# Sums of weights for a seven-product scheme on one Trainium2 core: one accumulating DMA and GpSimd additions in place of three accumulating DMAs, with the feed-forward in three parts

## The chip, the core and the metric

The kernel runs on one core of a Trainium2 chip. The metric is the device time of one execution in microseconds; for a comparison several executions are timed and their median is taken. Beside the timed runs, one execution is recorded by the hardware profiler; every line number and duration below is from that record. Engines are TensorE (PE, with its weight loads PEld), VectorE (DVE), ScalarE (ACT), GpSimd (POOL) and SyncE (SP), each with a queue of its own that is worked off in order.

## What is computed

A decoder trunk of two layers on 512 tokens of width 1024, all in float32. Each layer is a feed-forward, a token mixer and a second feed-forward, added to the residual stream. The change concerns the four feed-forwards only:

```
def swiglu(h, w_gate, w_up, w_down):
    return (jax.nn.silu(h @ w_gate) * (h @ w_up)) @ w_down

for l in range(2):
    x = x + 0.5 * swiglu(rms_norm(x, ffn1_norm[l]), ffn1_w_gate[l], ffn1_w_up[l], ffn1_w_down[l])
    ...                       # mixer: causal convolution and differential attention
    x = x + 0.5 * swiglu(rms_norm(x, ffn2_norm[l]), ffn2_w_gate[l], ffn2_w_up[l], ffn2_w_down[l])
```

The hidden width is 2816, which is 22 tiles of 128.

## The kernel before, in words

The residual stream x lies in SBUF with features on partitions: eight tiles (KT) of 128 features by 512 tokens. Every product is made from split operands: a value is rounded to a shorter float (hi) and its remainder kept (lo), and three matmuls, hi·hi, hi·lo and lo·hi, stand for one (`mm3`, lines 136 to 142). Weights are split on the chip: `parts_of` (93 to 95) lets ScalarE write hi (L94) and VectorE write lo (L95).

A feed-forward (`ffn`, 341 to 401) goes through its 22 hidden tiles in two halves of 11. For each tile it makes gate and up outputs, applies silu and the product, and splits the result into `hh` and `hl` (`gated`, L358 and L359). After 11 tiles comes a down pass: for each of the 8 output tiles, 11 hidden tiles times three matmuls accumulate in a bank `ps_d`, which L399 adds to x. Its weights come in chunks of eight blocks of 128x128 (L397).

The first three tiles (PLAIN) are made by plain products. The other 19 tiles of a feed-forward, a pair of gate and up each, go through `seven` (304 to 339): the pair's 2 by 2 block product is made from seven products in place of eight, each over four feature tiles, so 7 × 4 × 3 = 84 matmuls of 256 tokens. It needs sums of weight blocks (g1, g2 are the halves of the gate weights, u1, u2 of the up weights): g1, g2, u2, g1+u1, u2+u1, g1+u2+u1, and the sum of all four; the signs are in the activations and in the last step. It also needs sums of activations, made once a feed-forward by `Halves` (267 to 302): whole normalized tiles `hn`, sums `ht` by GpSimd (L284, L285) and VectorE, split into `th` and `tl`; `settle` splits the whole tiles into `acth` and `actl`. Each of the seven products goes to a quarter of two PSUM banks: a and d are halves of the first, c and b of the second. Between the products the running sum of a bank's half is copied out by ScalarE (L323 to L329) or added by VectorE (L331 to L338) to tiles `g` and `n` in SBUF.

The sums of weights are made by `sums` (109 to 134). SP loads g1 and u2 into one buffer `raw`, which is split; then GpSimd issues a DMA that adds u1 to both halves in the buffer (`add_into`, L107), which is split again; a second accumulating DMA adds g1 to one half, which is split; a third adds g2 to it, which is split. So a pair has three accumulating DMAs, each changing a buffer that must have been read. The buffers are rings: three `wraw` of 128x1024, of which a pair takes one, four `whi` and four `wlo`, of which a pair takes three each; and two smaller ones each for g2 (`wraw2`, `whi2`, `wlo2`).

The order of instructions on each engine is fixed at build time by a scheduler that works with modelled durations; only the first matmul of each of the seven products is pinned to its place. An engine waits at its next instruction until what this one needs is there, whatever stands behind it. Bank pairs for the seven products take turns through three tags (`pair_banks`, 262 to 264), one of which (`mm`) also gives the two `ps_d` banks.

## Time and profile before

| | |
|---|---|
| time, median of 3 runs | 2290.9 us (2290.48 to 2295.74) |
| the profiled execution | 2303.2 us, of which 2301.1 us are its span |
| TensorE busy, mean granted clock | 1940.3 us (84%), 0.942 of full speed |
| VectorE, ScalarE, GpSimd busy | 1182.6, 917.9, 595.9 us |
| DMA | 236.49 MB, 103 GB/s over the span |
| accumulating DMAs on GpSimd's queue | 228: 76 of 512 KB, 152 of 256 KB |
| chain that ended last | PE 39%, DMA 30% (loads and accumulations of gate and up weights), DVE 13%, ACT 6%, issue 6% |

How to read the lines that follow. A group of the profile reads: line, engine, operation, output<-inputs, shapes, count | busy us and mean ns of one | idle time of the engine just before these instructions and what ended it. A line of waits reads: engine, tile and line that waited <- what it waited for: us in total, times, longest. A line of a timeline reads: start in us from the span's start, duration, engine, line, operation, [idle before <- what ended it]. A line of windows reads: stretch, length, busy time of PE, PEld, DVE, ACT and POOL with counts, granted TensorE clock (PEclk), DMA share, GB/s. Matmuls overlap one another, so that the time from one start to the next, not the duration, is the pace.

### The profile page before, as it was taken

The page shows a single profiled execution, that of the slowest core. Times are in us where ns is not written, and L with a number is a line of the kernel's source. Part 1 is how long each engine was busy: PE and PEld are TensorE (multiplying, and loading weights), DVE is VectorE, ACT ScalarE, POOL GpSimd, SP SyncE. Part 2 cuts the span into 40 slices and gives each one's busy share as a digit, 9 for nine tenths or more (in the row PEclk, how much of TensorE's full clock was granted, in tenths as well). Part 3 has the DMA queues.
Part 4 walks back from the last instruction along what each step waited for, and adds up shares of the span by engine and source line. Part 5 has one row for each costly group of instructions (what it writes and reads, how often), then busy time and mean ns, then how long its engine had stood idle before and what let it go on. Part 6 is the DMA issues. An engine that isn't in the chain of part 4 may idle for free.

```text
span 2301.1 us, 28742 instructions
## 1 busy us (share of the span) xinstructions
PE 1940.3 (84%) x11124; PEld 1703.9 (74%) x11124; DVE 1182.6 (51%) x1848; ACT 917.9 (40%) x1532; POOL 595.9 (26%) x500
## 2 busy tenths in 40 slices
PE   7678877899998879777987797679999987897789
PEld 5667776788787768767877687677887867777677
DVE  7444344548869443344474443444488674424442
ACT  5333233335745342333433322333458444313331
POOL 4110111119934110111121101121397421101110
PEclk9799999999998999899998999999999999999899
DMA  5455365532213554455425544555321245535542
GB/s 158 111 120 126 76 123 103 136 101 83 83 37 83 115 120 108 98 110 115 128 60 109 115 121 83 118 104 133 95 87 56 65 91 111 128 92 106 108 105 89
DMA packets 104088, 236.49 MB, mean 103 GB/s; under 512 B 11271, under 2 KB 11430, under 8 KB 103952
## 3 DMA queue, kind: packets, MB, share of 16 engines
q0 software_dynamic: 44192, 82.51, 22.6%
q1 hardware_dynamic: 59616, 152.07, 21.3%
q8 instruction: 87, 1.43, 0.2%
q14 instruction: 49, 0.40, 0.1%
q10 hardware_dynamic: 144, 0.08, 0.0%
HBM read 232.51 MB, written 3.42 MB: 103 GB/s over the span
## 4 chain that ended last, share of the span: by engine, by line
PE 39%; DMA 30%; DVE 13%; issue 6%; ACT 6%; POOL 0%; ACTq 0%; POOLq 0%; SPq 0%; DVEq 0%
DMA wraw<-in_gu 30%; DVE wlo L95 7%; PE ps_d L138 6%; PE ps_d L142 6%; PE ps_d L141 6%; ACT whi L94 6%; PE ps_pair L318 6%; PE ps_pair L141 2%; PE ps_pair L142 2%; PE ps_pair L138 2%; PE ps_pair L518 1%; PE ps_pair L517 1%; PE ps_pair L516 1%; PE ps_out L141 1%; PE ps_sc L634 1%
## 5 line engine op out<-in xcount | busy, mean ns | idle before, releaser
L95 DVE TENSOR_TENSOR wlo<-wraw,whi 128x512 fp32r<-128x512 f32 (+1 forms) x506 | 500.5, 993 | 657.1 <-ACT whi L94 645.4
L94 ACT ACTIVATE whi<-wraw 128x1024 fp32r<-128x1024 f32 (+1 forms) x550 | 467.8, 873 | 891.3 <-DMA wraw<-in_gu 539.9
L107 POOL DMA_DIRECT2D wraw<-in_gu x228 | 223.4, 981 | 1277.1 <-DVE wlo L95 1198.4
L318 PE MATMUL ps_pair<-acth,whi 128*128 128x256 f32 x1216 | 373.8, 307 | 151.7 <-DVE g L331 138.9
L318 PE MATMUL ps_pair<-th,whi 128*128 128x256 f32 x912 | 293.4, 322 | 158.1 <-ACT n L325 76.7
L318 PEld LDWEIGHTS ps_pair<-acth,whi 128*128 128x128 f32 x1216 | 255.8, 210 | 167.2 <-ACT whi L94 130.9
L318 PE MATMUL ps_pair<-actl,whi 128*128 128x256 f32 x1216 | 367.9, 303 | 10.2 <-DVE actl L295 10.2
L318 PE MATMUL ps_pair<-acth,wlo 128*128 128x256 f32 x1216 | 366.1, 301 | 0.3 <-DVE wlo L95 0.3
L318 PEld LDWEIGHTS ps_pair<-th,whi 128*128 128x128 f32 x912 | 196.3, 215 | 184.8 <-ACT n L325 87.3
L138 PE MATMUL ps_d<-hh,whi 128*128 128x512 f32 x704 | 276.0, 394 | 16.4 <-ACT whi L94 13.8
L318 PE MATMUL ps_pair<-tl,whi 128*128 128x256 f32 x912 | 280.3, 307 | 10.5 <-DVE tl L289 10.5
L318 PE MATMUL ps_pair<-th,wlo 128*128 128x256 f32 x912 | 277.4, 304 | 0.2 <-DVE wlo L95 0.2
L141 PE MATMUL ps_d<-hl,whi 128*128 128x512 f32 x704 | 274.7, 390 | 0.0
L142 PE MATMUL ps_d<-hh,wlo 128*128 128x512 f32 x704 | 273.3, 390 | 0.0
L318 PEld LDWEIGHTS ps_pair<-actl,whi 128*128 128x128 f32 x1216 | 256.6, 211 | 13.4 <-DVE actl L295 12.4
L318 PEld LDWEIGHTS ps_pair<-acth,wlo 128*128 128x128 f32 x1216 | 256.6, 211 | 0.6 <-DVE wlo L95 0.5
L318 PEld LDWEIGHTS ps_pair<-tl,whi 128*128 128x128 f32 x912 | 196.0, 215 | 14.0 <-DVE tl L289 13.6
L318 PEld LDWEIGHTS ps_pair<-th,wlo 128*128 128x128 f32 x912 | 195.1, 214 | 0.7 <-DVE wlo L95 0.7
L138 PEld LDWEIGHTS ps_d<-hh,whi 128*128 128x128 f32 x704 | 132.5, 188 | 50.9 <-ACT whi L94 18.9
L142 PEld LDWEIGHTS ps_d<-hh,wlo 128*128 128x128 f32 x704 | 132.7, 189 | 27.5
L141 PEld LDWEIGHTS ps_d<-hl,whi 128*128 128x128 f32 x704 | 132.5, 188 | 26.2
L138 PE MATMUL ps_pair<-acth,whi 128*128 128x512 f32 x320 | 125.6, 397 | 6.0 <-ACT whi L94 6.0
(175 smaller groups left out, 2880.9 us busy)
## 6 DMA issues: line engine op xcount, KB each, us to landing
wraw<-in_gu SPq DMA_DIRECT2D x232, 256.0 KB, 3.5
wraw<-in_dn SPq DMA_DIRECT2D x88, 512.0 KB, 3.9
wraw<-in_gu POOLq DMA_DIRECT2D x76, 512.0 KB, 6.1
wraw<-in_gu POOLq DMA_DIRECT2D x152, 256.0 KB, 4.2
wraw<-in_wqkv SPq DMA_DIRECT2D x24, 512.0 KB, 3.6
wraw<-in_gu SPq DMA_DIRECT2D x22, 512.0 KB, 3.6
wraw<-in_wag SPq DMA_DIRECT2D x16, 512.0 KB, 3.7
wraw<-in_wout SPq DMA_DIRECT2D x16, 512.0 KB, 3.6
```

The source lines that it names most:

```text
L94: S.activation(hi, raw, AF.Copy)
L95: (eng or V).tensor_tensor(out=lo, in0=raw, in1=f32(hi), op=ALU.subtract)
L107: nc.gpsimd.dma_start(dst, src, accum_op=ALU.add)
L138: first = T.matmul(ps, wh, xh, start=start, stop=False)
L141: T.matmul(ps, wh, xl, start=False, stop=False)
L142: T.matmul(ps, wl, xh, start=False, stop=stop)
L318: mm = T.matmul(ps, l, r, start=first and i == j == 0, stop=False, skip_group_check=True)
L516: T.matmul(ps[n], xh[:, t], wh, start=k == 0, stop=False)
L517: T.matmul(ps[n], xh[:, t], wl, start=False, stop=False)
L518: T.matmul(ps[n], xl[:, t], wh, start=False, stop=k == KT - 1)
L634: T.matmul(scs[m], qz[:, m, h, tq], kt[:, h, :W], start=True, stop=True)
```

## The change

Three things are changed, all in the feed-forwards.

The sums. A pair now loads g whole (`whole`), g1 and u2 into a second buffer (`two`), and u2 once more into the small ring. One accumulating DMA adds u1 to both halves of `two`. GpSimd then makes g1+u2+u1 and the sum of all with two `tensor_tensor` additions into a third buffer (`more`). A pair takes three `wraw` buffers, of which there are now five. Splits are in another order: whole (g1, g2), u2u1, g1u2u1, u2, all, g1u1.

The parts. The 22 tiles go in three parts of 8, 8 and 6 tiles with a down pass after each. The array of down weights in memory stays laid out for two halves of 11, so `gather` puts a chunk of eight blocks together from two to four loads (a few chunks are one load). Temporary sums `ht` of `Halves` take turns in two buffers in place of four.

The products. Their order becomes g1, u2u1, g2, g1u2u1, u2, all, g1u1, with b and c exchanged in the second bank. The sums of products and the gate are made in the PSUM banks by VectorE, and silu and the split read them there.

In the changed kernel, line numbers are higher: L95 becomes L97 and L94 L96, L107 becomes L140, the additions are L145 and L146, the matmuls L318 become L343, the copies of a, c, a, d out of the banks are L348, L350, L353 and L355, and loads of down weights are L117.

```diff
@@ -40,6 +40,8 @@
 STATS_AT = 5
 
 PLAIN = 3
+
+PARTS = ((0, 8), (8, 8), (16, 6))
 HS = SEQ // 2
 
 SPACE = 392
@@ -84,7 +86,7 @@
         return psum.tile([P, 512], F32, tag=tag, name=name, bufs=BANKS[tag])
 
 
-    RING = {"wraw": 3, "whi": 4, "wlo": 4, "wraw2": 2, "whi2": 2, "wlo2": 2}
+    RING = {"wraw": 5, "whi": 4, "wlo": 4, "wraw2": 2, "whi2": 2, "wlo2": 2}
 
     def ring(tag, n=1024):
         dt = F32 if "raw" in tag else F32R
@@ -103,34 +105,56 @@
             parts_of(raw[:, s], hi[:, s], lo[:, s], eng)
         return hi, lo
 
-    def add_into(dst, src):
-        nc.gpsimd.dma_start(dst, src, accum_op=ALU.add)
+    def gather(src, blocks, eng=None):
+
+        raw, hi, lo = ring("wraw"), ring("whi"), ring("wlo")
+        n = 0
+        while n < len(blocks):
+            (half, b), w = blocks[n], 1
+            while (b + w) % 8 and n + w < len(blocks) and blocks[n + w] == (half, b + w):
+                w += 1
+            c = b % 8
+            nc.sync.dma_start(raw[:, n * P : (n + w) * P], src[half, b // 8][:, c * P : (c + w) * P])
+            n += w
+        c = slice(0, len(blocks) * P)
+        parts_of(raw[:, c], hi[:, c], lo[:, c], eng)
+        return hi, lo
 
     def sums(g, u):
 
-
         h = slice(0, 512), slice(512, 1024)
-        raw = ring("wraw")
-        nc.sync.dma_start(raw[:, h[0]], g[:, h[0]])
-        nc.sync.dma_start(raw[:, h[1]], u[:, h[1]])
         w = {}
 
-        def give(names, t, raw):
-            parts_of(raw, *t)
-            for n, name in enumerate(names):
-                w[name] = tuple(p[:, n * 512 : (n + 1) * 512] for p in t)
-
-        give(("g1", "u2"), (ring("whi"), ring("wlo")), raw)
-        raw2 = ring("wraw2", 512)
-        nc.sync.dma_start(raw2, g[:, h[1]])
-        add_into(raw.rearrange("p (b c) -> p b c", b=2), u[:, h[0]].unsqueeze(1).broadcast_to([P, 2, 512]))
-        give(("g1u1", "u2u1"), (ring("whi"), ring("wlo")), raw)
-        last = ring("whi"), ring("wlo")
-        add_into(raw[:, h[1]], g[:, h[0]])
-        give(("g1u2u1",), tuple(p[:, h[0]] for p in last), raw[:, h[1]])
-        give(("g2",), (ring("whi2", 512), ring("wlo2", 512)), raw2)
-        add_into(raw[:, h[1]], g[:, h[1]])
-        give(("all",), tuple(p[:, h[1]] for p in last), raw[:, h[1]])
+        def give(name, t, n, raw):
+            w[name] = tuple(p[:, h[n]] for p in t)
+            parts_of(raw, *w[name])
+
+        whole = ring("wraw")
+        nc.sync.dma_start(whole, g)
+        two = ring("wraw")
+        nc.sync.dma_start(two[:, h[0]], g[:, h[0]])
+        nc.sync.dma_start(two[:, h[1]], u[:, h[1]])
+        u2 = ring("wraw2", 512)
+        nc.sync.dma_start(u2, u[:, h[1]])
+
+        nc.gpsimd.dma_start(
+            two.rearrange("p (b c) -> p b c", b=2), u[:, h[0]].unsqueeze(1).broadcast_to([P, 2, 512]), accum_op=ALU.add
+        )
+
+        more = ring("wraw")
+        G.tensor_tensor(more[:, h[0]], two[:, h[1]], whole[:, h[0]], op=ALU.add)
+        G.tensor_tensor(more[:, h[1]], more[:, h[0]], whole[:, h[1]], op=ALU.add)
+        t = ring("whi"), ring("wlo")
+        parts_of(whole, *t)
+        for n, name in enumerate(("g1", "g2")):
+            w[name] = tuple(p[:, h[n]] for p in t)
+        t = ring("whi"), ring("wlo")
+        give("u2u1", t, 0, two[:, h[1]])
+        give("g1u2u1", t, 1, more[:, h[0]])
+        give("u2", (ring("whi2", 512), ring("wlo2", 512)), 0, u2)
+        t = ring("whi"), ring("wlo")
+        give("all", t, 0, more[:, h[1]])
+        give("g1u1", t, 1, two[:, h[0]])
         return w
 
     def mm3(ps, w, x, start, stop, pin=False):
@@ -274,13 +298,14 @@
             self.tl = fp.tile([P, 3, KT // 2, HS], F32R, tag="tl", name="tl")
 
             self.whole = []
+            free = [f"hh{n}" for n in range(PLAIN, 8)] + [f"hl{n}" for n in range(PLAIN, 6)]
             a, b = slice(0, HS), slice(HS, SEQ)
             for j in range(KT // 2):
-                ha, hb = (fp.tile([P, SEQ], F32, tag=f"hh{PLAIN + i}", name="hn") for i in (j, j + KT // 2))
+                ha, hb = (fp.tile([P, SEQ], F32, tag=free[i], name="hn") for i in (2 * j, 2 * j + 1))
                 for k, h in ((j, ha), (j + KT // 2, hb)):
                     V.scalar_tensor_tensor(h, x[:, k, :], col(pr.l, pr.gain, k), r, op0=ALU.mult, op1=ALU.mult)
                     self.whole.append((k, h))
-                t = fp.tile([P, 4, HS], F32, tag=f"hl{PLAIN + 2 * j}", name="ht")[:, :3]
+                t = fp.tile([P, 3 + j % 2, HS], F32, tag=("ht", "hl6")[j % 2], name="ht")[:, :3]
                 G.tensor_tensor(t[:, 1], hb[:, b], ha[:, b], op=ALU.subtract)
                 G.tensor_tensor(ha[:, b], ha[:, a], ha[:, b], op=ALU.subtract)
                 V.scalar_tensor_tensor(t[:, 0], ha[:, b], -1.0, hb[:, b], op0=ALU.mult, op1=ALU.subtract)
@@ -304,7 +329,7 @@
     def seven(halves, w, banks, fp):
 
         a, d = banks[0][:, :HS], banks[0][:, HS:]
-        c, b = banks[1][:, :HS], banks[1][:, HS:]
+        b, c = banks[1][:, :HS], banks[1][:, HS:]
         g = fp.tile([P, SEQ], F32, tag="g", name="g", bufs=2)
         n = fp.tile([P, SEQ], F32, tag="n", name="n", bufs=2)
 
@@ -321,46 +346,43 @@
 
         go(a, "g1", "b11", first=True)
         S.activation(g[:, :HS], a, AF.Copy)
+        go(c, "u2u1", "t1", first=True)
+        S.activation(n[:, HS:], c, AF.Copy)
+        go(b, "g2", "b21")
+        go(a, "g1u2u1", "t2")
+        S.activation(g[:, HS:], a, AF.Copy)
         go(d, "u2", "t4")
         S.activation(n[:, :HS], d, AF.Copy)
-        go(c, "u2u1", "t1", first=True)
-        S.activation(n[:, HS:], c, AF.Copy)
-        go(a, "g1u2u1", "t2")
-        S.activation(g[:, HS:], a, AF.Copy)
-        go(b, "g2", "b21")
-        V.tensor_tensor(g[:, :HS], b, g[:, :HS], op=ALU.add)
         go(c, "all", "b22")
-        V.tensor_tensor(g[:, HS:], c, g[:, HS:], op=ALU.add)
-        S.activation(g, g, AF.Silu)
+        V.tensor_tensor(banks[1], banks[1], g, op=ALU.add)
+        S.activation(g, banks[1], AF.Silu)
         go(a, "g1u1", "t3")
-        V.tensor_tensor(n[:, HS:], a, n[:, HS:], op=ALU.add)
-        V.tensor_tensor(n[:, :HS], a, n[:, :HS], op=ALU.add)
-        V.scalar_tensor_tensor(n, n, -1.0, g, op0=ALU.mult, op1=ALU.mult)
-        return n
+        V.tensor_tensor(d, a, n[:, HS:], op=ALU.add)
+        V.tensor_tensor(a, a, n[:, :HS], op=ALU.add)
+        V.scalar_tensor_tensor(banks[0], banks[0], -1.0, g, op0=ALU.mult, op1=ALU.mult)
+        return banks[0]
 
     def ffn(pr, gu, dn, after, lead=None, aside=None):
         with tc.tile_pool(name="ffn", bufs=1) as fp:
             r = halves = None
-            for half in range(2):
-                hh, hl = [], []
-                held = []
+            for m0, many in PARTS:
+                hh, held, more = [], [], []
 
                 def gated(n, us):
                     hi = fp.tile([P, SEQ], F32R, tag=f"hh{n}", name="hh")
-                    if n < PLAIN:
+                    if n < 6:
                         lo = fp.tile([P, SEQ], F32R, tag=f"hl{n}", name="hl")
-                    elif (n - PLAIN) % 2 == 0:
-                        two = fp.tile([P, 2, SEQ], F32R, tag=f"hl{n}", name="hl")
-                        lo = two[:, 0]
-                        hl.append(two[:, 1])
+                    elif n == 6:
+                        two = fp.tile([P, 2, SEQ], F32R, tag="hl6", name="hl")
+                        lo, more[:] = two[:, 0], [two[:, 1]]
                     else:
-                        lo = hl.pop()
+                        lo = more.pop()
                     S.activation(hi, us, AF.Copy)
                     V.tensor_tensor(lo, us, f32(hi), op=ALU.subtract)
                     hh.append((hi, lo))
 
-                for mm in range(HALF):
-                    m = half * HALF + mm
+                for mm in range(many):
+                    m = m0 + mm
                     if m == 4 and aside:
                         aside()
                     if m >= PLAIN:
@@ -388,16 +410,18 @@
                         V.tensor_tensor(us, us, gs, op=ALU.mult)
                         gated(n, us)
                     held = []
+                blocks = [divmod(m0 + kk, HALF) for kk in range(many)]
+                blocks = [(half, m * HALF + f) for m in range(KT) for half, f in blocks]
                 w = None
                 for m in range(KT):
                     ps = bank("mm", "ps_d")
-                    for kk in range(HALF):
-                        b = m * HALF + kk
+                    for kk in range(many):
+                        b = m * many + kk
                         if b % 8 == 0:
-                            w = chunk(dn[half, b // 8])
-                        mm3(ps, wpart(w, b % 8), hh[kk], kk == 0, kk == HALF - 1)
+                            w = gather(dn, blocks[b : b + 8])
+                        mm3(ps, wpart(w, b % 8), hh[kk], kk == 0, kk == many - 1)
                     V.scalar_tensor_tensor(x[:, m, :], ps, 0.5, x[:, m, :], op0=ALU.mult, op1=ALU.add)
-                    if half == 1:
+                    if m0 + many == FT:
                         after(m)
```

## The prediction

> **What bounds the kernel now.** I read the page's head first, then the waits, then GpSimd's timeline through one pair.
>
> ```profile
> span 2301.1 us, 28742 instructions
> ...
> PE 1940.3 (84%) x11124; PEld 1703.9 (74%) x11124; DVE 1182.6 (51%) x1848; ACT 917.9 (40%) x1532; POOL 595.9 (26%) x500
> ```
>
> The profiled execution has a span of 2301.1 us. TensorE looks 84% busy, but matmuls overlap in this column, so I go by start times below.
>
> ```profile
> POOL wraw L107 <- DVE wlo L95: 1198.4, 221, 53.8
> ...
> ACT whi L94 <- DMA wraw<-in_gu: 539.9, 222, 7.5
> ...
> PE ps_pair L318 <- DVE g L331: 138.9, 64, 3.9
> ```
>
> GpSimd spends 1198.4 us, half the span, in front of its accumulating DMAs (L107), waiting for VectorE to have finished with the buffer that the DMA changes; ScalarE then waits 539.9 us for DMAs of gate and up weights. These two waits follow one another, and the timeline of GpSimd shows how.
>
> ```profile
> 162.39 1.20 POOL L107 DMA_DIRECT2D wraw<-in_gu  x1 [0.63 <-DVE wlo L95]
> 171.18 0.88 POOL L107 DMA_DIRECT2D wraw<-in_gu  x1 [7.59 <-DVE wlo L95]
> 177.17 0.85 POOL L107 DMA_DIRECT2D wraw<-in_gu  x1 [5.11 <-DVE wlo L95]
> 178.66 1.20 POOL L107 DMA_DIRECT2D wraw<-in_gu  x1 [0.63 <-DVE wlo L95]
> ```
>
> The four rows are one turn of the pair's three accumulating DMAs: the broadcast one at 162.39, the second at 171.18, the third at 177.17, and the next pair's first at 178.66. That is a period of 16.27 us. Each DMA may start only after the one before has landed and its result has been split (L94, L95), and GpSimd's queue keeps them in one row. Landing times are in the DMA part of the page:
>
> ```profile
> wraw<-in_dn SPq DMA_DIRECT2D x88, 512.0 KB, 3.9
> wraw<-in_gu POOLq DMA_DIRECT2D x76, 512.0 KB, 6.1
> wraw<-in_gu POOLq DMA_DIRECT2D x152, 256.0 KB, 4.2
> ```
>
> 8.79 us from first to second is the 6.1 us landing plus a split; 5.99 from second to third is 4.2 plus a shorter split; 1.5 closes the turn. So the serial chain of DMAs on GpSimd's queue sets about 16.3 us for a pair, and TensorE's own work does not.
>
> TensorE's own need comes from its rows: within a product, matmuls start 0.12 us apart (171.18, 171.30).
>
> ```profile
> 171.18 0.28 PE L318 MATMUL ps_pair<-actl,whi 128*128 128x256 f32 x1
> 171.30 0.28 PE L318 MATMUL ps_pair<-acth,wlo 128*128 128x256 f32 x1
> 172.11 0.38 PE L318 MATMUL ps_pair<-th,whi 128*128 128x256 f32 x1 [0.53 <-ACT g L323]
> 172.33 0.28 PE L318 MATMUL ps_pair<-tl,whi 128*128 128x256 f32 x1
> ```
>
> 84 matmuls in a pair make 84 × 0.12 = 10.1 us, 6 us below the period.
>
> The four feed-forward stages, from the first matmul of tile 3 to the last down matmul, and the pace of down matmuls:
>
> ```profile
> 45.90:499.50 453.60, 357.00 (x2129) 320.49 (x2128) 202.72 (x298) 163.14 (x267) 71.16 (x73) 0.92 0.50 111
> 731.30:1161.00 429.70, 349.07 (x2125) 314.88 (x2124) 195.51 (x280) 157.74 (x259) 62.89 (x62) 0.93 0.50 111
> 1194.60:1633.80 439.20, 351.85 (x2125) 318.38 (x2124) 193.13 (x274) 157.75 (x258) 63.40 (x62) 0.92 0.49 109
> 1865.50:2297.40 431.90, 349.08 (x2125) 314.90 (x2124) 184.53 (x269) 145.48 (x239) 54.04 (x56) 0.93 0.48 105
> sum 1754.40, PE 1407.00 PEld 1268.64 DVE 775.90 ACT 624.12 POOL 251.49; mean PE 351.75 PEld 317.16 DVE 193.97 ACT 156.03 POOL 62.87
> ```
>
> ```profile
> L138 PE MATMUL ps_d<-hh,whi x77: 389/389/499, 869.8 to 922.1; 128*128 128x512 f32 x77
> ```
>
> The first column after the stretch is its length: 1754.4 us of 2301.1 are these stages. The ps_d row gives 77 groups of three from 869.8 to 922.1, so 0.230 us a matmul; 4 × 528 down matmuls (8 outputs × 22 tiles × 3) are 486 us. Of the starts of the stages I keep 50 us, an estimate: TensorE stands there until VectorE has made the sums of activations.
>
> ```profile
> 739.09 0.58 PE L318 MATMUL ps_pair<-th,whi 128*128 128x256 f32 x1 [3.00 <-ACT th L288]
> 743.50 0.58 PE L318 MATMUL ps_pair<-tl,whi 128*128 128x256 f32 x1 [3.83 <-DVE tl L289]
> ```
>
> These two idles are 6.8 us in one stage, smaller ones and half-clock stretches lie beside them, and the first stage starts more slowly; about 12 us each. That leaves 1754 − 486 − 50 = 1218 us for 76 pairs, 16.0 each, which agrees with 16.27 in mid-part.
>
> **The change, part by part.**
>
> *One accumulating DMA a pair.* Two of the three accumulating DMAs go; their sums become two GpSimd additions of 128x512. The trace has such additions elsewhere:
>
> ```profile
> L95 DVE TENSOR_TENSOR wlo<-wraw,whi 128x1024 fp32r<-128x1024 f32 x274 | 341.7, 1251 | 248.6 <-ACT whi L94 238.1 <-PE ps_pair L318 7.1 <-PE ps_pair L141 3.1
> ...
> L95 DVE TENSOR_TENSOR wlo<-wraw,whi 128x512 fp32r<-128x512 f32 x232 | 159.6, 689 | 408.5 <-ACT whi L94 407.3
> ...
> L588 POOL TENSOR_TENSOR yp<-yp,prod 128x512 f32<-128x512 f32 x78 | 100.7, 1292 | 7.2 <-ACT prod L587 4.4
> L232 POOL TENSOR_TENSOR ssum<-ssum,sq 128x512 f32<-128x512 f32 x42 | 66.2, 1577 | 210.3 <-ACT sq L231 209.4
> ```
>
> 1.29 us (L588) to 1.58 us (L232) each. In the built kernel's order GpSimd issues the DMA of a pair, both additions, then the next pair's DMA, so its queue needs 6.1 + 2 × 1.29 to 2 × 1.58, plus perhaps 0.3 of signals: 9.0 to 9.6 us a pair. It falls below TensorE's 10.1. The data no longer wait on splits between the DMAs: whole, two and u2 arrive from SP, and only the one DMA and the additions follow. By the ring of five buffers the loads for pair n+2 may start when pair n's last split is done, about three quarters through pair n−1's matmuls; until those results are needed early in pair n+1 there are some 22 us at 13 us a pair, and load, DMA and additions need 3.9 + 6.1 + 3.2 + signals, 14. So DMA leaves the path, with 8 us to spare. SP issues four loads a pair in place of three; nothing waits for that while the spare lasts.
>
> The longer duration of L232 is of additions beside two-input VectorE work. The Trainium skill (SBUF — State Buffer, Who interferes with whom) says a VectorE instruction with two SBUF inputs and a GpSimd instruction that reads SBUF block each other wholly. By that page, two additions would hold VectorE for up to 2 × 1.29 = 2.6 us a pair, an estimate; the 1.58 against 1.29 agrees in kind.
>
> VectorE's work in a pair is 1.25 + 5 × 0.69 for splits and about 2.9 for the rest (four rows like those of 170.80 to 173.04 below, and a 0.69 for the gate), 7.6 us. Were it held for the whole of both additions, 2 × 1.29 (L588), it would need 10.2, still below 13. I take nothing for it and keep 0 to 1 us a pair in the range.
>
> *What is late next: TensorE and ScalarE.* The matmuls of one PSUM bank wait for a copy out of the other half of that bank (both kernels show it in their waits). After the change the order is g1, u2u1, g2, g1u2u1, u2, all, g1u1. Two of them wait: g2 for the copy of u2u1's result (same bank), u2 for the copy of a after g1u2u1. The other copies lie beside a product that uses the other bank.
>
> ```profile
> 165.20 1.15 ACT L94 ACTIVATE whi<-wraw 128x512 fp32r<-128x512 f32 x2 [1.34 <-DMA wraw<-in_gu]
> ...
> 171.67 0.38 ACT L323 ACTIVATE g<-ps_pair 128x256 f32<-128x256 f32 x1 [1.53 <-PE ps_pair L318]
> 172.38 0.63 ACT L358 ACTIVATE hh<-n 128x512 fp32r<-128x512 f32 x1 [0.32 <-DVE n L338]
> ```
>
> The shortest such wait is in the rows: last matmul at 171.30, copy 171.67 to 172.05, next matmul 172.11 in place of 171.42, and one more 0.1 lost to the second (172.33). So 0.69 + 0.1 = 0.8 us. That is g2's.
>
> u2's wait is longer, because ScalarE's order in the built kernel puts four splits of the next pair ahead of that copy, two of which need g2 finished and two g1u2u1 finished (their buffers come free there). Counted from the start of g2's last matmul: ScalarE starts 0.37 later, two splits take 1.15 (row 165.20), to 1.52; g1u2u1's last matmul starts at 1.44, so the next two splits run from 1.81 to 2.96, the copy to 3.34, TensorE resumes at 3.40 where it could have at 1.56. That is 1.84 + 0.1 = 1.9 us. A pair then needs 10.1 + 0.8 + 1.9 = 12.8 us. It replaces the waits of before, among them those for g at L331 (138.9 us, also a bank shared with a reader), which go with the sum in PSUM.
>
> *The clock.* In the rows below, stretches of 3.41 us follow each other; PEclk is the column before DMA share.
>
> ```profile
> 417.98:421.39 3.41, 1.70 (x15) 1.49 (x13) 0.52 (x1) 1.53 (x3) 1.01 (x1) 1.00 0.87 135
> 421.39:424.80 3.41, 2.76 (x23) 2.79 (x24) 1.53 (x4) 0.75 (x1) 0.00 (x0) 1.00 1.03 262
> 305.34:308.75 3.41, 1.50 (x13) 1.33 (x12) 1.53 (x3) 1.42 (x3) 0.44 (x1) 1.00 0.90 136
> 308.75:312.16 3.41, 3.41 (x18) 3.41 (x18) 1.23 (x3) 1.69 (x2) 0.00 (x0) 0.50 0.99 275
> ```
>
> With TensorE busy 1.50 of 3.41 the next stretch ran at 0.50; busy 1.70, at 1.00. The wait of 1.84 us, if it falls within one stretch, leaves some 1.7 busy: on the edge. A halved stretch costs up to 1.7 us. I take one pair in eight, 0.2 a pair: 13.0 us.
>
> The Trainium skill (TensorE: Matmul & The Clock Gate, What's actually happening) has the clock fall after at least one idle window of about 3.4 us; by that rule waits of 1.9 us never halve it, the pair would stay at 12.8 and the sum be 15 us lower. The trace disagrees, since 305.34 was 44% busy.
>
> *Three parts.* Twelve ends of parts in place of eight. At an end, down matmuls fill the last pair's two waits (worth 2.7 us), but of the 48 matmuls of the first two outputs (there are two banks) six need the last tile itself. With eight tiles 42 are ready, and in the built order all of them stand ahead of the last pair's last three products. So after the last product TensorE waits for the chain of sums, product and split.
>
> ```profile
> 170.80 0.42 DVE L336 TENSOR_TENSOR n<-ps_pair,n 128x256 f32<-128x256 f32 x1
> ...
> 173.04 0.69 DVE L359 TENSOR_TENSOR hl<-n,hh 128x512 fp32r<-128x512 f32 x1 [0.70 <-ACT hh L358]
> ```
>
> From 170.80 to the end of hh (172.38 + 0.63) are 2.2 us; with signals 2.5 of idle, then about 0.8 until hl and the next bank are there, and a halved stretch of 1.7: 5.0 − 2.7 = 2.3 us, times 12 is 28 us. Before, 11 tiles left more down matmuls over and this was near nothing. Down products keep number and pace. Their loads grow from 88 to 216 smaller ones (counted in the built order); a chunk of eight blocks feeds 24 matmuls, 5.5 us, against 3.9 to land, with five buffers: nothing, unless they queue (below). GpSimd's first additions now stand ahead of the sums of activations at a stage's start, which may cost some 3 us; tile 3 needs them two products later, which gives 24 × 0.12 = 2.9 back.
>
> *Sums in PSUM, order of b and c.* Same counts and shapes for VectorE; nothing on the path beyond what is above.
>
> **The sum.** 486 + 50 + 76 × 13.0 + 28 = 1552, against 1754: 202 us less. The profiled execution took 2303.2 us, 0.5% above the median of 2290.9, so 2290.9 − 202 = 2089, say 2090. A difference of 0.3% is about what can be told from none here.
>
> **Rivals.**
>
> - *Denser.* If the copy ahead of u2 didn't stand behind the splits, both waits would be 0.8: 11.7 a pair, 76 × 1.3 = 99 less, 1990. The ScalarE order speaks against it. 0.10.
> - *Clock.* Each pair loses a stretch: 12.8 + 1.7 = 14.5, 114 more, 2204. The row at 44% speaks for it, that at 50% against. 0.16.
> - *Down loads, slower.* SP starts 128 more DMAs, of rows as short as 512 bytes, and a chunk of two to four must all land. At the 3.9 us landing in series, 2.45 × 3.9 = 9.6 us a chunk against 5.5: 88 × 4.1 = 360 more, 2450, slower. It decides from about 202 / 88 = 2.3 us beyond the cover of a chunk. Against: loads of 512 KB land in 3.9, so landing is mostly fixed time and overlaps. 0.07.
> - *No gain.* The one accumulating DMA, now among more SP loads, lands so late that GpSimd's queue again takes 16 us (it would need to land in 13, against 6.1): about 2290. 0.03.
>
> My forecast has 0.64. The range 2030 to 2215 takes in the forecast from 12.2 to 13.8 us a pair and the clock's case, 0.80; it leaves out the denser case, the slow loads and no gain. Faster 0.90, same 0.02, slower 0.08.
>
> **What would show it.** Right: the waits list loses its 1198 us of GpSimd for VectorE as a part of the chain, DMAs leave the chain of waits, silu to silu in mid-part is near 13 us, TensorE's idle ahead of L343 is two waits a pair, 0.8 and 1.9, both ended by ScalarE, and GpSimd additions last 1.3 to 1.6. Wrong: ScalarE waiting for in_gu DMAs within a pair, PEclk of 0.5 in most pairs, gaps in the down rows ended by in_dn, or idles at part ends well off 3.3 us.

## The result, and the profile after

| | before | after |
|---|---|---|
| median of the runs side by side | 2293.3 us (4 runs) | 2118.5 us (2115.5 to 2126.5, 4 runs) |
| the profiled execution, its span | 2303.2, 2301.1 us | 2115.5, 2113.7 us |
| mean granted clock | 0.942 | 0.967 |
| one pair in mid-part, silu to silu, mean | 16.2 us (56) | 12.5 us (48) |
| first of the seven products to tile 3's silu, four stages | 47.5, 23.7, 26.4, 23.3 us | 46.3, 36.5, 34.1, 36.5 us |

The ratio is 0.924 (95% interval 0.921 to 0.927): 188 us less between the two profiled executions, 175 by the medians, where 202 was forecast. The last two rows are worked out from the starts of all silu instructions (L334, now L358); pairs next to a start or to an end of a part are left out of the mean.

The head and the chain of the page of after:

```profile
span 2113.7 us, 29273 instructions
...
PE 1850.3 (88%) x11124; PEld 1620.0 (77%) x11124; DVE 1270.9 (60%) x1880; ACT 932.1 (44%) x1608; POOL 675.9 (32%) x500
...
PE 81%; DVE 6%; ACT 5%; issue 3%; DMA 2%; POOL 1%; ACTq 0%; SPq 0%; DVEq 0%; POOLq 0%
```

DMA has fallen from 30% of the chain to 2%, TensorE has risen from 39% to 81%. The waits of after:

```profile
POOL wraw L140 <- DMA wraw<-in_gu: 485.9, 31, 44.6
...
PE ps_pair L343 <- ACT g L353: 91.9, 63, 1.7
...
POOL wraw L140 <- DVE wlo L97: 67.0, 12, 6.2
...
PE ps_pair L343 <- ACT acth L319: 65.5, 8, 13.8
...
PE ps_d L162 <- ACT hh L380: 30.3, 12, 2.8
...
PE ps_pair L343 <- ACT n L350: 29.5, 62, 0.5
```

GpSimd's 1198 us in front of its DMAs for VectorE's splits have shrunk to 67; it now stands mostly for loads that have not come yet, and TensorE is not late for that in mid-part. TensorE's own list has four long entries: two waits a pair (L353 ahead of u2, L350 ahead of g2), one at each end of a part (L380), and eight long ones at the starts of stages (L319). TensorE through one pair, only the rows with a wait:

```profile
347.05 0.39 PE L343 MATMUL ps_pair<-th,whi 128*128 128x256 f32 x1 [1.44 <-ACT g L353]
354.98 0.38 PE L343 MATMUL ps_pair<-acth,whi 128*128 128x256 f32 x1 [0.47 <-ACT n L350]
359.56 0.38 PE L343 MATMUL ps_pair<-th,whi 128*128 128x256 f32 x1 [1.45 <-ACT g L353]
```

From u2 to u2 are 12.51 us. The matmuls before these rows start at 345.33 and 354.23; less the usual 0.12 and with 0.1 lost at the next matmul, the waits cost 1.7 and 0.7, and 10.1 + 1.7 + 0.7 is the pair. The four stages (length, then busy time of each engine):

```profile
45.67:448.50 402.83, 333.27 (x2129) 297.99 (x2130) 225.23 (x305) 167.90 (x286) 92.53 (x74) 0.94 0.46 125
679.36:1070.10 390.74, 330.02 (x2131) 296.44 (x2130) 221.85 (x291) 165.21 (x282) 80.48 (x61) 0.96 0.45 122
1102.55:1489.60 387.05, 330.10 (x2126) 297.27 (x2125) 215.64 (x287) 161.85 (x278) 82.22 (x61) 0.96 0.46 123
1720.58:2110.00 389.42, 329.06 (x2125) 295.10 (x2123) 209.33 (x280) 152.61 (x263) 72.36 (x55) 0.96 0.42 114
sum 1570.04, PE 1322.45 PEld 1186.80 DVE 872.05 ACT 647.57 POOL 327.59; mean PE 330.61 PEld 296.70 DVE 218.01 ACT 161.89 POOL 81.90
```

1570 us, where the sum of the prediction had 1552 and before had 1754: 184 of the 187 us between the two spans lie in these stages.

At the start of a stage something new stands out. TensorE and GpSimd in the second stage, after the norm has been spread:

```profile
682.35 0.39 PE L343 MATMUL ps_pair<-actl,whi 128*128 128x256 f32 x1 [0.32 <-DVE actl L320]
682.57 0.28 PE L343 MATMUL ps_pair<-acth,wlo 128*128 128x256 f32 x1
696.01 0.58 PE L343 MATMUL ps_pair<-acth,whi 128*128 128x256 f32 x1 [13.15 <-ACT acth L319]
```

```profile
678.54 0.73 POOL L310 TENSOR_TENSOR hn<-hn 128x256 f32<-128x256 f32 x1
692.53 1.20 POOL L140 DMA_DIRECT2D wraw<-in_gu  x1 [13.26 <-DVE tl L314]
693.30 1.19 POOL L309 TENSOR_TENSOR ht<-hn 128x256 f32<-128x256 f32 x1
```

TensorE stands for 13.2 us within tile 3's second product, and the granted clock is at half from 683.3 to 707.1 us. GpSimd has done four of the eight subtractions for the sums of activations by 679.3, then its queue stands at the accumulating DMA of tile 5, and the fifth subtraction (L309) follows only at 693.30. Either the DMA holds the queue, or the subtraction itself could not have gone before, because its temporary `ht` has two buffers in place of four. That is taken apart below.

### The profile page after: what moved, and what is told of

Its sections match the earlier page's. It is cut to its first block, busy times and chain, and to the rows that moved or that the text cites. A ratio compares the mean times of both kernels' runs of the same rounds, so it can differ in the third digit from the quotient of the medians.

```text
span 2113.7 us, 29273 instructions
## 1 busy us (share of the span) xinstructions
PE 1850.3 (88%) x11124; PEld 1620.0 (77%) x11124; DVE 1270.9 (60%) x1880; ACT 932.1 (44%) x1608; POOL 675.9 (32%) x500
## 4 chain that ended last, share of the span: by engine, by line
PE 81%; DVE 6%; ACT 5%; issue 3%; DMA 2%; POOL 1%; ACTq 0%; SPq 0%; DVEq 0%; POOLq 0%
PE ps_pair L343 37%; PE ps_d L165 8%; PE ps_d L166 8%; PE ps_d L162 8%; ACT whi L96 3%; PE ps_pair L162 2%; PE ps_pair L165 2%; PE ps_pair L166 2%; DMA wraw<-in_gu 2%; DVE wlo L97 1%; PE ps_out L165 1%; PE ps_out L162 1%; PE ps_out L166 1%; PE ps_pair L540 1%; PE ps_pair L541 1%
## 5 line engine op out<-in xcount | busy, mean ns | idle before, releaser
L97 DVE TENSOR_TENSOR wlo<-wraw,whi 128x512 fp32r<-128x512 f32 (+1 forms) x582 | 557.6, 983 | 400.8 <-ACT whi L96 400.4
L96 ACT ACTIVATE whi<-wraw 128x512 fp32r<-128x512 f32 (+1 forms) x626 | 479.4, 792 | 698.1 <-PE ps_pair L343 344.9
L343 PE MATMUL ps_pair<-acth,whi 128*128 128x256 f32 x1216 | 355.7, 293 | 95.8 <-ACT acth L319 65.5
L343 PE MATMUL ps_pair<-actl,whi 128*128 128x256 f32 x1216 | 350.4, 288 | 22.7 <-DVE actl L320 22.7
L343 PE MATMUL ps_pair<-acth,wlo 128*128 128x256 f32 x1216 | 348.1, 286 | 0.5 <-DVE wlo L97 0.5
L343 PE MATMUL ps_pair<-th,whi 128*128 128x256 f32 x912 | 264.5, 290 | 92.2 <-ACT g L353 91.9
L343 PEld LDWEIGHTS ps_pair<-acth,whi 128*128 128x128 f32 x1216 | 236.4, 195 | 113.1 <-ACT acth L319 68.2
L140 POOL DMA_DIRECT2D wraw<-in_gu x76 | 91.7, 1207 | 721.8 <-DMA wraw<-in_gu 485.9
L162 PE MATMUL ps_d<-hh,whi 128*128 128x512 f32 x704 | 279.4, 400 | 32.1 <-ACT hh L380 30.3
L343 PEld LDWEIGHTS ps_pair<-actl,whi 128*128 128x128 f32 x1216 | 236.9, 195 | 27.7 <-DVE actl L320 26.9
L343 PE MATMUL ps_pair<-tl,whi 128*128 128x256 f32 x912 | 258.0, 283 | 0.0
L343 PE MATMUL ps_pair<-th,wlo 128*128 128x256 f32 x912 | 257.6, 283 | 0.0
L343 PEld LDWEIGHTS ps_pair<-th,whi 128*128 128x128 f32 x912 | 174.4, 191 | 105.8 <-ACT g L353 104.8
L343 PEld LDWEIGHTS ps_pair<-acth,wlo 128*128 128x128 f32 x1216 | 237.2, 195 | 0.8 <-DVE wlo L97 0.8
L145 POOL TENSOR_TENSOR wraw<-wraw 128x512 f32<-128x512 f32 x76 | 104.6, 1377 | 334.9 <-DMA wraw<-in_gu 225.0
L423 DVE SCALAR_TENSOR_TENSOR x<-ps_d,x 128x512 f32<-128x512 f32 x96 | 66.1, 690 | 199.8 <-PE ps_d L166 199.8
L343 PEld LDWEIGHTS ps_pair<-tl,whi 128*128 128x128 f32 x912 | 174.7, 192 | 0.5
L343 PEld LDWEIGHTS ps_pair<-th,wlo 128*128 128x128 f32 x912 | 174.6, 191 | 0.0
```

Source lines behind the costliest of these rows:

```text
L96: S.activation(hi, raw, AF.Copy)
L97: (eng or V).tensor_tensor(out=lo, in0=raw, in1=f32(hi), op=ALU.subtract)
L140: nc.gpsimd.dma_start(two.rearrange("p (b c) -> p b c", b=2), u[:, h[0]].unsqueeze(1).broadcast_to([P, 2, 512]), accum_op=ALU.add)
L145: G.tensor_tensor(more[:, h[0]], two[:, h[1]], whole[:, h[0]], op=ALU.add)
L162: first = T.matmul(ps, wh, xh, start=start, stop=False)
L343: mm = T.matmul(ps, l, r, start=first and i == j == 0, stop=False, skip_group_check=True)
```

## The experiments

Theory: the gain is that of the shorter chain of DMAs; what is left of a pair is ScalarE's order; the dear starts come from `ht`. The rivals were the sums in PSUM with the new order of products, and the queue of GpSimd. All ratios are to the kernel before on the same chip. The kernel before took 2293.3 us beside the changed kernel and 2299.0 to 2302.1 beside the others, so that a difference of medians between the first row and another can be off by some 9 us; the ratios are free of that. The start column is the sum over the four stages.

| kernel | median us | ratio, 95% interval | starts | pair, mean |
|---|---|---|---|---|
| changed kernel | 2118.5 | 0.921 to 0.927 | 153.4 | 12.5 |
| three DMAs back | 2369.5 | 1.026 to 1.035 | 135.2 | 17.0 |
| sums alone on the kernel before | 2106.5 | 0.912 to 0.917 | 126.4 | 13.3 |
| copy of a first | 2062.4 | 0.893 to 0.898 | 153.5 | 11.3 |
| four `ht` | 2088.8 | 0.905 to 0.909 | 120.1 | 12.5 |
| queue order alone | 2102.7 | 0.912 to 0.917 | 135.5 | 12.5 |
| four `wraw` | 2205.2 | 0.952 to 0.964 | 156.7 | 14.2 |
| two halves, four `wraw` | 2221.0 | 0.962 to 0.968 | 146.1 | 14.4 |
| two halves, copy first, four `ht` | 2147.7 | 0.931 to 0.936 | 114.2 | 13.6 |
| copy first, four `ht` | 2026.3 | 0.879 to 0.883 | 118.0 | 11.4 |
| old order of products | 2105.3 | 0.912 to 0.918 | 156.3 | 11.9 |
| swapped, pinned, four `ht` | 1926.2 | 0.836 to 0.840 | 120.4 | 9.95 |
| swapped, four `ht` | 1938.5 | 0.841 to 0.844 | 119.9 | 10.3 |

**Three DMAs back.** In the changed kernel `sums` is that of before:

```diff
-        nc.gpsimd.dma_start(
-            two.rearrange("p (b c) -> p b c", b=2), u[:, h[0]].unsqueeze(1).broadcast_to([P, 2, 512]), accum_op=ALU.add
-        )
...
-        G.tensor_tensor(more[:, h[0]], two[:, h[1]], whole[:, h[0]], op=ALU.add)
-        G.tensor_tensor(more[:, h[1]], more[:, h[0]], whole[:, h[1]], op=ALU.add)
+        add_into(raw.rearrange("p (b c) -> p b c", b=2), u[:, h[0]].unsqueeze(1).broadcast_to([P, 2, 512]))
...
+        add_into(raw[:, h[1]], g[:, h[0]])
...
+        add_into(raw[:, h[1]], g[:, h[1]])
```

> The changed kernel with the three accumulating DMAs of before put back into the sums; the three parts, the new order of products and the sums in PSUM stay. Theory: the whole gain comes from the chain of DMAs on GpSimd's queue, so a pair goes back from 12.5 to about 16.0 to 16.3 us, 76 x 3.5 to 3.8 more: 2380 to 2405 us, slower than before, since three parts and the dearer starts of stages stay. Rival: the order of products and the sums in PSUM make the gain; then the pair stays at 12.5 to 13 us and the time below 2160.

Measured: 17.0 us a pair, more than the 16.3 expected, and 2369.5 us, less than the 2380 expected; slower than before by 3.1%. Its waits:

```profile
POOL wraw L124 <- DVE wlo L97: 1418.0, 224, 38.5
```

The old wait of GpSimd for VectorE is back, larger than before. So the chain of DMAs carries the gain, and without it the rest of the change costs 3%.

**The sums alone.** The kernel before with the new `sums`, four `wraw` for three, and the split of u2 second:

```diff
-    RING = {"wraw": 3, "whi": 4, "wlo": 4, "wraw2": 2, "whi2": 2, "wlo2": 2}
+    RING = {"wraw": 4, "whi": 4, "wlo": 4, "wraw2": 2, "whi2": 2, "wlo2": 2}
```

> The kernel before with the new sums alone (one accumulating DMA, two GpSimd additions, four weight buffers, and the split of u2 put second as its product comes second there); two halves of 11, the old order of products and the sums in SBUF stay. Theory: without the chain of DMAs TensorE's waits for its banks set the pair, two waits of 0.8 us at the least and 1.9 for one of them at the most: 11.7 to 12.8 us a pair, 76 x 3.2 to 4.3 under the kernel before: 1970 to 2050 us; that is below the changed kernel, since it has fewer ends of parts and four buffers for the sums of activations. Rival: the new order and the sums in PSUM are needed for the gain; then TensorE waits for VectorE at the additions of g and a pair keeps 14 us or more: above 2140.

Measured: 2106.5 us. The rival falls; this one part gives more than the whole change, by ratios whose intervals lie apart. But a pair takes 13.3, not 11.7 to 12.8. The longest wait of TensorE:

```profile
PE ps_pair L325 <- DVE g L338: 109.4, 67, 3.6
```

That is 1.6 us each time, where 0.8 was put. The runs of four `wraw` and of the old order below point to the four buffers: with five, this wait is 1.0 us and the pair 11.9. That comparison is not clean, since the old order below has three parts as well.

**The copy of a first.** A dependency that only orders ScalarE puts the splits of `all` and `g1u1` behind the copy (L353) that u2 waits for:

```diff
+LATE = ("all", "g1u1")
...
-        S.activation(hi, raw, AF.Copy)
+        ins = S.activation(hi, raw, AF.Copy)
+        if late and copied:
+            behind(ins, copied[-1])
...
-        S.activation(g[:, HS:], a, AF.Copy)
+        copied.append(S.activation(g[:, HS:], a, AF.Copy))
```

> The changed kernel with one order on ScalarE pinned: the splits of the sums all and g1+u1 of the next pair stand behind the copy of a that u2 waits for, so that two splits in place of four are ahead of it. Theory: those splits make u2's wait 1.7 us in place of 0.8; the pair goes from 12.5 to about 11.6, in the 64 pairs that do not end a part: 58 us less, 2050 to 2065 us. Rival: the wait is that of the copy behind the product itself, or another engine is next (GpSimd's queue, VectorE's splits); then the pair stays above 12.2 and the time within 20 us of the changed kernel.

Measured: 2062.4 us. The wait for the copy (here L364):

```profile
PE ps_pair L354 <- ACT g L364: 30.0, 63, 0.7
```

It was 91.9 us in 63 waits and is now 30.0 in 63. Splits of the next pair ahead of a copy were what made 0.5 into 1.5 of idle; that is shown.

**Four buffers for `ht`**, room for them from a pad:

```diff
-                t = fp.tile([P, 3 + j % 2, HS], F32, tag=("ht", "hl6")[j % 2], name="ht")[:, :3]
+                t = fp.tile([P, 3 + (j == 1), HS], F32, tag=("ht", "hl6", "ht2", "ht3")[j], name="ht")[:, :3]
```

> The changed kernel with four buffers for the temporary sums of activations in place of two (room taken from a pad). Theory: the two buffers, with the next pair's accumulating DMA behind them on GpSimd's queue, hold back the third and fourth sums, and so the second product of tile 3, by 13 us in three of the four stages: the time from the first of the seven products to tile 3's silu falls from 36.5 to about 24 us, 36 us less in all, 2075 to 2090 us. Rival: VectorE, which has no idle from the spread of the norm to the splits of these sums, sets the start, and order and buffers change little: within 8 us of the changed kernel.

Measured: 2088.8 us; starts 120.1 in place of 153.4, as in the kernel before (120.9). With four buffers the scheduler also puts all eight subtractions ahead of tile 5's DMA, so this alone does not part buffer from queue.

**The queue order alone.** Two buffers, tile 5's DMA behind the eight subtractions:

```diff
-        nc.gpsimd.dma_start(
+        add = nc.gpsimd.dma_start(
...
+        if late:
+            behind(add, made[-1])
```

> The changed kernel with GpSimd's order alone altered: the accumulating DMA of tile 5 stands behind all eight GpSimd subtractions for the sums of activations, in place of between the fourth and the fifth; the temporary sums keep two buffers. Theory: the two buffers are enough to hold the third sum back (its buffer comes free only when the first sum's second split is done, 1 us before the point at which the DMA lets the queue go), so the start stays at 36.5 us from the first product to tile 3's silu and the time within 8 us of the changed kernel. Rival: the DMA's place in the queue is the cause; then the start falls to about 27 us, as with four buffers, and the time by 25 to 30 us.

Measured: 2102.7 us, starts 135.5: 18 of the 33 us, neither of the two sizes expected. GpSimd in the second stage (L319, L320 are the subtractions here):

```profile
674.13 0.74 POOL L320 TENSOR_TENSOR hn<-hn 128x256 f32<-128x256 f32 x1
687.27 1.38 POOL L319 TENSOR_TENSOR ht<-hn 128x256 f32<-128x256 f32 x1 [12.40 <-DVE tl L324]
```

With nothing ahead of it the fifth subtraction still waits 12.4 us for VectorE's split `tl` of the first sum: the buffer does hold it. The DMA's place added to that: in the changed kernel the load that it needs was issued at 687.59 us and landed at 691.96, and the DMA left the queue at 692.53. Both are causes, 18 us by the queue and the other 15 by the buffers, taken in this order.

**Four `wraw`** in place of five in the changed kernel:

```diff
-    RING = {"wraw": 5, "whi": 4, "wlo": 4, "wraw2": 2, "whi2": 2, "wlo2": 2}
+    RING = {"wraw": 4, "whi": 4, "wlo": 4, "wraw2": 2, "whi2": 2, "wlo2": 2}
```

> The changed kernel with four weight buffers of 128x1024 in place of five, nothing else. Theory: a load, the DMA and two additions have about 8 us of spare at a pair of 12.5 us, so one buffer less is hidden and the pair stays at 12.5 us: within 10 us of the changed kernel. Rival: the fifth buffer is what lets the loads run ahead; then ScalarE waits for gate and up weights in mid-part and the pair goes to 13.5 us or more, 76 us or more in all.

Measured: 2205.2 us. The theory falls: one buffer is worth 87 us by the medians, 79 by the ratios. ScalarE, then TensorE, three windows, GpSimd and SP in a slow pair:

```profile
242.78 0.63 ACT L96 ACTIVATE whi<-wraw 128x512 fp32r<-128x512 f32 x1 [2.58 <-DMA wraw<-in_gu]
244.14 0.63 ACT L96 ACTIVATE whi<-wraw 128x512 fp32r<-128x512 f32 x1 [0.73 <-POOL wraw L145]
245.81 1.15 ACT L96 ACTIVATE whi<-wraw 128x512 fp32r<-128x512 f32 x2 [1.04 <-POOL wraw L146]
246.87 0.36 ACT L353 ACTIVATE g<-ps_pair 128x256 f32<-128x256 f32 x1
```

```profile
247.28 0.58 PE L343 MATMUL ps_pair<-th,whi 128*128 128x256 f32 x1 [3.90 <-ACT g L353]
```

```profile
241.80:245.20 3.40, 1.58 (x14) 1.38 (x12) 1.61 (x2) 1.26 (x2) 2.28 (x2) 1.00 0.01 2
245.20:248.60 3.40, 1.32 (x6) 1.32 (x7) 2.42 (x3) 1.42 (x3) 0.58 (x1) 0.51 0.45 131
248.60:252.00 3.40, 3.40 (x18) 3.40 (x18) 0.69 (x1) 0.90 (x2) 1.20 (x1) 0.50 0.62 178
```

```profile
234.78 1.19 POOL L140 DMA_DIRECT2D wraw<-in_gu  x1 [4.47 <-DMA wraw<-in_gu]
...
244.19 1.59 POOL L146 TENSOR_TENSOR wraw<-wraw 128x512 f32<-128x512 f32 x1
250.14 1.20 POOL L140 DMA_DIRECT2D wraw<-in_gu  x1 [4.37 <-DMA wraw<-in_gu]
```

```profile
245.80 0.33 SPq L135 DMA_DIRECT2D wraw<-in_gu  x1
```

The four splits belong to the next pair and are late, because its DMA is late. They stand ahead of the present pair's copy of a, so TensorE waits 3.9 us for data that it does not need yet; and the clock, after a stretch busy 1.58 of 3.40, is halved for two stretches. The load for the DMA at 250.14 starts at 245.80, when GpSimd's second addition (from 244.19, 1.59 long) has set a buffer free: a loop of load, DMA and two additions, 15.4 us from one DMA to the next. With the fifth buffer the pair is 12.5 us again.

**Two halves** of 11 in the changed kernel, with four `wraw` to make room:

```diff
-PARTS = ((0, 8), (8, 8), (16, 6))
+PARTS = ((0, 11), (11, 11))
```

> The changed kernel with two halves of 11 tiles in place of three parts, and four weight buffers of 128x1024 to make room; sums, order of products, PSUM sums and two buffers for the temporary sums of activations stay. Theory: an end of a part of 8 costs about 2.6 us and one of 11 about 0.5, so twelve ends at 28 us become eight at 4: 24 us less than the kernel of the same call with four buffers and three parts, about 2092 us. Rival: the ends are hidden, or many small loads of down weights cost something else: then either within 5 us of it, or more than 45 us less.

Measured: 2221.0 us, not 24 less than three parts with four `wraw`; the 16 more are not clear of noise, since the intervals of the two ratios overlap. The ends in its waits, and all the waits of down matmuls for another engine in the sums alone, which also has two halves:

```profile
PE ps_d L162 <- ACT hh L380: 27.8, 8, 3.5
```

```profile
PE ps_d L145 <- DVE x L406: 2.6, 8, 0.3
```

3.5 us at each of eight ends against 2.5 at each of twelve (30.3 us). Neither the number of tiles nor the pace explains this: the sums alone, with shorter pairs (13.3 us against 14.4), has no wait for `hh` at its ends. By the rows it is the order on TensorE. Down matmuls from the first one to the last pair's last product, in this kernel and in the sums alone:

```profile
184.00:205.90 21.90, 14.20 (x60) 11.07 (x60) 0.00 (x0) 1.00 0.33 108
```

```profile
172.00:192.15 20.15, 10.30 (x43) 7.93 (x44) 0.00 (x0) 1.00 0.45 145
```

Of the 66 down matmuls of the first two outputs (11 tiles times three, twice), 60 do not need the last tile. Here all 60 stand ahead of the last product, at seven of the eight ends, and none are left to fill the wait behind it; in the sums alone 43 stand ahead at seven of eight (33 in the kernel before), and the rest fill it. So three parts cost no more than two halves in the order as built, and they leave room for the fifth `wraw`. Two halves with five were not run.

**Together**, with two halves:

```diff
+LATE = ("all", "g1u1")
+PARTS = ((0, 11), (11, 11))
...
+    RING = {"wraw": 4, "whi": 4, "wlo": 4, "wraw2": 2, "whi2": 2, "wlo2": 2}
...
+                t = fp.tile([P, 4, HS], F32, tag=f"hl{PLAIN + 2 * j}", name="ht")[:, :3]
```

> What helped put together: the new sums, order and PSUM sums, two halves of 11, four weight buffers of 128x1024, four buffers for the temporary sums of activations, and the copy of a ahead of two splits on ScalarE. If the parts add up: the changed kernel's 2116 less 24 for the ends, 30 for the starts and 60 for the copy (68 pairs at 0.9): about 2000 us, 1990 to 2020. If they cover one another (a shorter pair leaves the next bound, the loads with four buffers): 2020 to 2060.

Measured: 2147.7 us and 13.6 us a pair, above both ranges. The next run, with five buffers, points to the four as the reason.

**Copy first and four `ht`**, with three parts and five `wraw`:

```diff
+LATE = ("all", "g1u1")
...
+                t = fp.tile([P, 3 + (j == 1), HS], F32, tag=("ht", "hl6", "ht2", "ht3")[j], name="ht")[:, :3]
```

> The changed kernel (three parts, five weight buffers) with both of the edits that helped: the copy of a ahead of two splits, and four buffers for the temporary sums of activations. Theory: one shortens the pairs, the other the starts, so they add up: 2116 - 56 - 30 = 2030 us, 2020 to 2040, and what held the same two edits with two halves back was their four weight buffers. Rival: with shorter pairs five weight buffers are too few as well; then 2050 us or more.

Measured: 2026.3 us. The two add up.

**The old order of products** and the sums in SBUF, in the changed kernel, with u2 split second:

```diff
-        go(c, "u2u1", "t1", first=True)
...
+        go(d, "u2", "t4")
+        S.activation(n[:, :HS], d, AF.Copy)
+        go(c, "u2u1", "t1", first=True)
```

> The changed kernel with the products of before: order g1, u2, u2+u1, g1+u2+u1, g2, all, g1+u1, sums of products in SBUF, and the split of u2 second; the new sums, three parts and five weight buffers stay. Theory: with the DMAs off the path the old order waits about as long as the new one; the pairs of 12.0 us that the new sums alone showed where buffers were not short are its pace: 64 x 0.5 less, 2075 to 2110 us. Rival: the sums in PSUM and the new order are worth something by themselves: then 13 us or more a pair, above 2140 us.

Measured: 2105.3 us, 11.9 us a pair. Sums in PSUM and the new order are worth nothing by themselves here, rather a loss of 0.6 us a pair. TensorE's wait for VectorE's addition is

```profile
PE ps_pair L343 <- DVE g L356: 63.6, 63, 2.9
```

1.0 us each, against 1.6 with four `wraw` in the sums alone.

**Swapped.** The two waits that are left come from a product that follows a product of the same bank. Making g1+u2+u1 ahead of g2 puts each copy beside a product of the other bank; four splits stand behind the copy of a, and `ht` has four buffers:

```diff
+LATE = ("u2u1", "g1u2u1", "all", "g1u1")
...
-        go(b, "g2", "b21")
         go(a, "g1u2u1", "t2")
-        S.activation(g[:, HS:], a, AF.Copy)
+        copied.append(S.activation(g[:, HS:], a, AF.Copy))
+        go(b, "g2", "b21")
```

> As the kernel with both edits, with g1+u2+u1 made ahead of g2 (order g1, u2+u1, g1+u2+u1, g2, u2, all, g1+u1), and all four splits of the next pair behind the copy of a on ScalarE. Theory: what is left of a pair over TensorE's 10.1 us is two waits of a product for a copy out of its own bank; in this order each copy lies beside a product of the other bank, and both waits go: 10.3 us a pair, 1.2 less in 64 pairs, 77 us less, 1945 to 1970 us. Rival: at that pace GpSimd's queue (one DMA and two additions, 9.0 to 9.6 us) or the loads behind it set the pair, at 11 us or more: 1990 to 2035 us.

Measured: 1926.2 us, better than the theory's range, and the best of all: 192 us less than the changed kernel by the medians. Its page, a stretch in mid-part, and its longest waits of TensorE:

```profile
PE 1823.2 (95%) x11124; PEld 1621.6 (85%) x11124; DVE 1241.1 (65%) x1880; ACT 928.3 (48%) x1608; POOL 675.4 (35%) x500
```

```profile
300.00:340.00 40.00, 40.00 (x319) 39.30 (x318) 25.32 (x38) 21.92 (x42) 13.32 (x10) 1.00 0.62 165
```

```profile
PE ps_d L173 <- ACT hh L391: 21.5, 12, 3.5
PE ps_pair L354 <- DVE tl L325: 19.4, 7, 5.2
```

TensorE has no idle in these 40 us, the clock is full, and neither GpSimd's queue nor the loads stop it at 10 us a pair; waits within pairs have left the list. At the ends of the parts of 8, eleven down matmuls now stand behind the last product, and the wait there is 1.0 us. The Trainium skill (Perfetto Trace Analysis, Matmuls) says that matmul groups should change banks so that one's eviction lies beside the next one's matmuls; by this run and the next the trace agrees. The order alone, with ScalarE's left to the scheduler, took the pair from 12.5 us (four `ht`) to 10.3 (the next run).

**Swapped, not pinned**, to part the order of products from that of ScalarE:

```diff
-LATE = ("u2u1", "g1u2u1", "all", "g1u1")
```

> As the swapped kernel (order g1, u2+u1, g1+u2+u1, g2, u2, all, g1+u1, and four buffers for the temporary sums of activations), but with ScalarE's order left to the scheduler. It puts two splits of the next pair, u2+u1 and g1+u2+u1, ahead of the copy of a, and these two need buffers that come free only when g2 is done. Theory: the wait at g2 goes, but u2 waits for g2's end, two splits (1.15 us) and the copy: 1.8 us as in the changed kernel; a pair takes 10.1 + 1.9 = 12.0 us against 11.5 with the copy pinned and the old place of g2, so 64 x 0.5 = 32 us more than that kernel's 2026: 2045 to 2075 us, 130 us above the swapped and pinned one. Rival: the order of products alone frees the copies; then 1930 to 1960 us.

Measured: 1938.5 us. The theory falls, and the rival holds. ScalarE in a pair:

```profile
322.20 0.38 ACT L350 ACTIVATE n<-ps_pair 128x256 f32<-128x256 f32 x1 [0.47 <-PE ps_pair L343]
323.52 1.15 ACT L96 ACTIVATE whi<-wraw 128x512 fp32r<-128x512 f32 x2 [0.94 <-PE ps_pair L343]
324.58 0.36 ACT L352 ACTIVATE g<-ps_pair 128x256 f32<-128x256 f32 x1
```

```profile
323.44 0.28 PE L343 MATMUL ps_pair<-acth,whi 128*128 128x256 f32 x1
...
324.99 0.39 PE L343 MATMUL ps_pair<-th,whi 128*128 128x256 f32 x1
```

The second fence is TensorE, the first matmuls of g2 and of u2. The two splits start when g2 has only begun, so what they waited for was g1+u2+u1: their buffers are not those that I had counted off. The copy of a is done by 324.94, and u2 starts 0.1 us later than at full pace. Against the kernel with four `ht` (2088.8), the order of products makes 150 us; the pinned splits add 12.

## Why the prediction was right, and where it was wrong

The forecast of 2090 us lies 28 below the measured 2118.5; the direction and the main cause are right. By its steps:

- *The bound before.* Right: three DMAs put back bring 17.0 us a pair back, the new sums alone take most of it away.
- *DMA leaves the path.* Right with five buffers. The 8 us to spare were not measured; with five buffers the chain stays off the path even at 9.95 us a pair, with four it is back in part, at some 80 us.
- *TensorE and ScalarE.* Right, with both sizes near: waits of 0.7 and 1.7 where 0.8 and 1.9 stood, 12.5 us a pair where 13.0 stood. That splits ahead of the copy make the longer one, the pinned copy has shown; *Denser*, for which the ScalarE order would have had to be otherwise, is that kernel (11.3).
- *The clock.* The rival falls: I count 12 drops to half speed in the trace of after against 59 before. Four of the 12 lie at the starts of stages and eight behind ends of parts, none in a pair in mid-part. So the 0.2 us a pair that the sum put for the clock, 15 us in all, did not come. The row quoted from the run with four `wraw` (46% busy, then halved) shows its mechanism with a wait of 3.9 us, the ends of parts with waits of 2.5.
- *VectorE and GpSimd.* The additions took what was put, 1.4 to 1.5 us, and lengthened VectorE's splits:

```profile
L97 DVE TENSOR_TENSOR wlo<-wraw,whi 128x512 fp32r<-128x512 f32 x384 | 307.0, 835 | 297.2 <-ACT whi L96 296.8
```

```profile
L146 POOL TENSOR_TENSOR wraw<-wraw 128x512 f32<-128x512 f32 x76 | 116.0, 1526 | 5.7
...
L145 POOL TENSOR_TENSOR wraw<-wraw 128x512 f32<-128x512 f32 x76 | 104.6, 1377 | 334.9 <-DMA wraw<-in_gu 225.0 <-DVE wlo L97 77.1 <-issue 17.8
```

  835 ns against 689 before and 693 with three DMAs back, 5 × 0.15 = 0.7 us a pair. TensorE did not wait for it, not even at 10 us a pair. The mean hides two cases: of the 384 splits, 280 meet no addition and take 690 ns, and 104 meet one and take 1226. A split that starts during an addition, from GpSimd and VectorE in one pair:

```profile
360.66 1.62 POOL L146 TENSOR_TENSOR wraw<-wraw 128x512 f32<-128x512 f32 x1
```

```profile
361.83 1.00 DVE L97 TENSOR_TENSOR wlo<-wraw,whi 128x512 fp32r<-128x512 f32 x1 [0.70 <-ACT whi L96]
```

  The addition ends at 362.28 and the split 0.55 us later, as it does in the median of the 74 such meetings; where the split is first, the addition ends 1.15 us behind it (median of 68), and an addition that meets no work of VectorE takes 1.29 (median of 25). So whichever comes second has most of its work still to do when the first one ends. The Trainium skill's full blocking (SBUF — State Buffer, Who interferes with whom) would have made up to 2.9 us a pair by these rows, an estimate, if both additions had held VectorE for their whole time. Where the two meet, the trace agrees with it; the price is 0.7 because three splits in four meet no addition.
- *Ends of parts.* Right in size (below), and the wait of 2.5 us is as put. That ends of 11 tiles cost near nothing held for the kernel before, because some of the ready down matmuls stood behind the last product there; in the new order none do with two halves, and those ends wait 3.5 us.
- *Down loads.* Right, nothing: in TensorE's list no down matmul waits for a weight, and ScalarE waits for in_dn once, 1.7 us.
- *Starts of stages left at 50.* This is the step that failed: "GpSimd's first additions now stand ahead of the sums of activations at a stage's start, which may cost some 3 us; tile 3 needs them two products later, which gives 24 × 0.12 = 2.9 back". From the first product to tile 3's silu the four starts take 153.4 us; less four pairs of 12.5 that is 103 in place of 50. 33 of it came with the change: `ht` in two buffers, which the text names as a change but never costs, and the accumulating DMA of tile 5 in GpSimd's queue. With four `ht` the starts are 120 us again, as before; and they stay at 120 when a pair takes 9.95. So of the other 20, some 15 are there because a start does not get shorter with the pairs (four times 3.7 us), while the sum took it so, and some 6 because the 50 was low: by the same count the starts of before are 120.9 less four pairs of 16.2, which is 56.

The sum with the measured terms: 486 + 103 + 76 × 12.5 + ends = 1570 leaves 31 for the ends (28 put). Starts +53, pairs −38, ends +3 make the 18 by which 1552 was short; outside the stages 3 us came back. That the stages came out so near is luck in part, since starts and pairs were wrong in opposite directions. The other half of the 28 is the base: the 202 were worked out on an execution of 2303.2 us and taken off a median of 2290.9, and the profiled execution of after lay 3 us under its own median.

Why the starts stay at 120 us I have only read from the trace and not tested: with four `ht`, VectorE shows no idle in the second stage from 662 to 696 us, that is from the spread of the norm to the splits of the sums.

## What to carry to other kernels

Once a chain of DMAs has left the path, look at what stands ahead of a copy out of PSUM in its engine's queue, and let neighbouring products use different banks: the two together took 2088.8 us (four `ht`) to 1926.2, nearly as much as the change itself had given. Cost every buffer that a change takes away, also those of small temporaries used once a stage, and every buffer that it adds: the fifth weight buffer alone held some 80 us. A price found in one order of instructions (ends of parts) or with one number of buffers (spare time of a DMA) is not the price in the next.
